# Attention's divisions, block turns and bias in another order, two heads turned by TensorE, and an MLP sum moved

## The chip, the cores and the metric

The kernel runs on one core of one Trainium2 chip. The metric is the device time in microseconds (us), median of several executions. TensorE (PE) multiplies, VectorE (DVE), ScalarE (ACT) and GpSimd (POOL) work element by element, and SyncE (SP) issues most transfers. POOL and ACT issue some too; transfers run on 16 shared engines.

## The reference, cut to what matters

A trunk of two layers on 512 tokens of width 1024. Each layer has a mixer and an MLP, each with a norm ahead of it and a residual addition behind.

```python
for layer in range(DEPTH):                       # DEPTH = 2
    hn = rmsnorm(h, norm_mix[layer])
    mix = attention(hn) if layer % 2 == 0 else rglru_block(hn)
    h = h + mix
    h = h + sq_relu_mlp(rmsnorm(h, norm_mlp[layer]), ...)   # relu(x @ w1)**2 @ w2
return rmsnorm(h, norm_final)

# attention: 16 heads of 64; a frame sees its own chunk of 64 and the 8 before it
s = einsum('bqhd,bkhd->bhqk', q_c, k_band) * scale + bias   # bias by clipped distance, per head
s = where(key_pos >= 0, s, NEG_INF)
p = softmax(s, axis=-1)
o = einsum('bhqk,bkhd->bqhd', p, v_band)                    # then o @ w_o
```

## The kernel before, in words

Everything is float32, and a product is made of three TensorE passes in float32r: each operand is split into a high part (a cast on ACT) and a low part (a subtraction on DVE), and high x high, high x low and low x high are added up in PSUM (`mm3`). So each weight tile that arrives costs ACT a cast `wh` and DVE a subtraction `wl` of 128 x 1024 before TensorE can use it.

Activations lie with channels in the partitions and the 512 tokens in the row. The program has three parts: attention (about the first 245 us), the first MLP, and the recurrent layer with the second MLP. The MLPs use sums of weight blocks and of activation blocks in place of one block product in eight; one such set of sums is `s1` to `s4` of a round.

In attention a head goes through these steps.
- `score(h)` (line 473): for four query tiles of 128, two matmuls each over the 128 to 512 keys up to the tile's end, into three PSUM banks; `K` and `Q` lie in both halves of the partitions, high part and low part, so that one pass of 128 rows gives two products. DVE adds the bias and takes the maximum (line 491), ACT takes the exponential and its sum (498), DVE the reciprocal, ACT divides (505).
- The block turn: DVE turns the 128 x 1280 probabilities in blocks of 32 x 32 (507), and sixteen transfers, eight on SP and eight on POOL (510), put the blocks where a full transpose would have them.
- `split_p(h)` (516): ACT casts the turned probabilities to the high part pH, DVE subtracts to get pL.
- `weigh(h)` (523): ten matmuls with V into one bank `oa`; ACT copies one half (`ax`), DVE adds (`o`); after the second head of a pair the pair is split into oH and oL.

Scores and `oa` take their banks from one set of four (`atp`), projections from another set of four (`mmp`).

What fills TensorE between heads is a queue of projections: V, the Q and K of pairs 2 to 7, and the output projection. Each is a generator that issues one `mm3` per step. `fill(n)` takes steps until a credit is used up, `need(name)` takes them until a projection is done. An entry of the queue may start only when a score or a weighting has been issued (`at["s"]`, `at["w"]`). `q_out` and `k_out` evacuate Q and K, and `k_out` copies the halves of K to the other partitions by four transfers on SP (kh and kl for two heads). The loop over `i` (617 to 641) issues score(i), a fill, split_p(i-2), weigh(i-3), a fill. A scheduler then sets the order on each engine from this, so the instruction order is not the order of the code.

The bias of four heads is one tile (373): one transfer of 512 KB, four copies and one memset on POOL.

In an MLP, `first` (797) runs the first up-projections, then calls `sums(0, False)`, `sums(0, True)` and `lengths()`; `sums(p, True)` makes the fourth sum of activations, s4, for the round, and `lengths` takes eight squared sums on ACT and four small instructions on DVE. `round_` (904) then takes its products in turn.

## Time and profile before

| | |
|---|---|
| median of 3 runs | 1033.38 us (1030.08 to 1033.62) |
| the profiled execution | 1030.76 us, span 1029.0 us |
| TensorE busy | 1006.7 us (98%), 5634 matmuls, mean granted clock 0.992 |
| VectorE busy | 865.8 us (84%) |
| ScalarE busy | 692.5 us (67%) |
| GpSimd busy | 163.4 us (16%) |
| mean HBM and on-chip transfer rate | 160 GB/s, 164.15 MB moved |

The span runs from the first to the last instruction; the execution is 1.8 us longer. Busy shares are averages over stages with different limits, so a stage is read by itself. A granted clock of 1.00 is TensorE's 2.4 GHz, of 0.50 its 1.2 GHz. A matmul counts as busy from its start to a modelled end, and matmuls overlap.

### The profile page before, as it was taken

To read this page: it belongs to the slowest core of one execution; us is meant where nothing else is said; L and a number is where in the kernel's file an instruction comes from. 1 tells how busy PE (TensorE), PEld (TensorE's weight loads), DVE (VectorE), ACT (ScalarE), POOL (GpSimd) and SP (SyncE) were. 2 spreads that over 40 slices of the span, in tenths; PEclk is the share of its full clock that TensorE was granted. 3 is DMA by queue.
4 is the path that set the end of the run, shared out by engine and by line. 5 is a ranking of instruction groups with operands and counts; after the bars stand their busy time and mean duration, and the time that the engine had idled before them with its cause. 6 is when DMAs were issued, how large, how long until landed. Compare 5 with 4: busy or idle time off the path is not lost.

```text
span 1029.0 us, 15661 instructions
## 1 busy us (share of the span) xinstructions
PE 1006.7 (98%) x5634; PEld 882.0 (86%) x5634; DVE 865.8 (84%) x1142; ACT 692.5 (67%) x1052; POOL 163.4 (16%) x256
## 2 busy tenths in 40 slices
PE   9998999979999999999999999999999999999997
PEld 8887788768989999999988788888999999999986
DVE  7899988759789898698688989987789798698687
ACT  7688988546786566567567686646686567567565
POOL 1053443313111111111020000003111111111020
PEclk9999999989999999999999999999999999999999
DMA  8476775549838738828673412186838838838572
GB/s 271 125 203 182 196 189 174 132 129 230 240 62 223 208 60 217 215 52 213 204 143 100 129 63 72 52 256 177 223 58 229 206 64 213 214 56 210 144 164 82
DMA packets 135725, 164.15 MB, mean 160 GB/s; under 512 B 10592, under 2 KB 102752, under 8 KB 135648
## 3 DMA queue, kind: packets, MB, share of 16 engines
q1 hardware_dynamic: 108896, 119.43, 37.4%
q0 software_dynamic: 26176, 43.01, 23.2%
q8 instruction: 44, 0.72, 0.3%
q10 hardware_dynamic: 576, 0.72, 0.2%
q14 instruction: 33, 0.27, 0.1%
HBM read 123.27 MB, written 2.10 MB: 122 GB/s over the span
## 4 chain that ended last, share of the span: by engine, by line
PE 75%; DVE 10%; ACT 6%; DMA 5%; issue 2%; SPq 1%; POOL 0%; DVEq 0%; ACTq 0%; POOLq 0%
PE m L290 8%; PE m L289 8%; PE m L288 8%; PE x L288 5%; PE x L289 5%; PE x L290 5%; PE y L289 4%; PE y L288 4%; PE y L290 4%; DVE wl L184 2%; DMA p<-pt 1%; DMA b<-in_w 1%; PE ro L290 1%; PE yb L290 1%; PE yb L288 1%
## 5 line engine op out<-in xcount | busy, mean ns | idle before, releaser
L184 DVE TENSOR_TENSOR wl<-b,wh 128x1024 fp32r<-128x1024 f32 x112 | 135.5, 1220 | 37.1 <-ACT wh L179 37.1
L179 ACT CAST wh<-b 128x1024 fp32r<-128x1024 f32 x112 | 116.7, 1051 | 61.5 <-PE m L289 19.1
L290 PE MATMUL m<-rH,wl 128*128 128x256 f32 x448 | 125.9, 281 | 0.0
L289 PE MATMUL m<-rL,wh 128*128 128x256 f32 x448 | 125.8, 281 | 0.0
L288 PE MATMUL m<-rH,wh 128*128 128x256 f32 x448 | 125.7, 281 | 0.0
L290 PE MATMUL m<-hnH,wl 128*128 128x256 f32 x336 | 95.0, 283 | 0.0
L289 PE MATMUL m<-hnL,wh 128*128 128x256 f32 x336 | 95.0, 283 | 0.0
L288 PE MATMUL m<-hnH,wh 128*128 128x256 f32 x336 | 94.9, 282 | 0.0
L179 ACT CAST wh<-wr 128x1024 fp32r<-128x1024 f32 (+1 forms) x65 | 66.6, 1028 | 38.1 <-PE ro L289 7.0
L289 PEld LDWEIGHTS m<-rL,wh 128*128 128x128 f32 x448 | 85.0, 190 | 1.2
L184 DVE TENSOR_TENSOR wl<-wr,wh 128x1024 fp32r<-128x1024 f32 (+1 forms) x66 | 77.9, 1184 | 9.3 <-ACT wh L179 9.0
L288 PEld LDWEIGHTS m<-rH,wh 128*128 128x128 f32 x448 | 84.8, 189 | 1.0
L290 PEld LDWEIGHTS m<-rH,wl 128*128 128x128 f32 x448 | 84.9, 189 | 0.0
L510 POOL DMA_DIRECT2D p<-pt x128 | 62.8, 499 | 121.8 <-DVE pt L507 70.1
L179 ACT CAST wh<-u 128x1024 fp32r<-128x1024 f32 x56 | 58.2, 1049 | 28.8 <-PE x L290 16.9
L184 DVE TENSOR_TENSOR wl<-u,wh 128x1024 fp32r<-128x1024 f32 x56 | 67.6, 1219 | 3.4 <-ACT wh L179 3.4
L289 PEld LDWEIGHTS m<-hnL,wh 128*128 128x128 f32 x336 | 64.3, 191 | 0.8
L288 PEld LDWEIGHTS m<-hnH,wh 128*128 128x128 f32 x336 | 64.2, 191 | 0.8
L290 PEld LDWEIGHTS m<-hnH,wl 128*128 128x128 f32 x336 | 64.3, 191 | 0.0
L136 POOL DMA_DIRECT2D kept<-in_w x14 | 18.3, 1308 | 261.0 <-DMA wr<-in_w 146.8
L163 POOL DMA_DIRECT2D u<-in_w x14 | 18.4, 1313 | 226.1 <-ACT m L853 117.2
L288 PE MATMUL x<-wh,h 128*128 128x512 f32 (+1 forms) x132 | 51.0, 386 | 0.6 <-DVE d L1062 0.6
(384 smaller groups left out, 3017.5 us busy)
## 6 DMA issues: line engine op xcount, KB each, us to landing
b<-in_w SPq DMA_DIRECT2D x68, 512.0 KB, 6.1
b<-b POOLq DMA_DIRECT2D x36, 512.0 KB, 6.5
kept<-in_w SPq DMA_DIRECT2D x28, 512.0 KB, 3.8
u<-in_w SPq DMA_DIRECT2D x28, 512.0 KB, 6.1
wr<-in_wqkv SPq DMA_DIRECT2D x20, 512.0 KB, 4.8
wr<-in_rwin SPq DMA_DIRECT2D x16, 512.0 KB, 3.6
kept<-in_w POOLq DMA_DIRECT2D x14, 512.0 KB, 7.2
u<-in_w POOLq DMA_DIRECT2D x14, 512.0 KB, 7.5
```

What stands on the lines that cost most here:

```text
L136: G.dma_start(four(raw), rows(upper[key]["22"]), accum_op=ALU.add)
L163: G.dma_start(four(raws["us3"]), rows(upper[key]["21"]), accum_op=ALU.add)
L179: high = S.copy(H[:, :n], raw[:, :n])
L184: low = V.tensor_sub(L[:, :n], raw[:, :n], f(H[:, :n]))
L288: PE.matmul(acc, WH, XH, start=start, stop=False, skip_group_check=more)
L289: PE.matmul(acc, WH, XL, start=False, stop=False, skip_group_check=more)
L290: PE.matmul(acc, WL, XH, start=False, stop=stop, skip_group_check=more)
L510: (G if j % 2 else nc.sync).dma_start(pt[32 * j : 32 * j + 32, i * 320 : (i + 1) * 320], turned[32 * i : 32 * i + 32, j].rearrange("p s a ...
```

## The change

Bias: a tile per head, with its own transfer, copy and memset; head i+3's is asked for in round i. In a round the order is now score(i), a fill, split_p(i-2), weigh(i-3), a fill, and then `divide(i)`: the division, the block turn and the sixteen transfers, which were part of `score` before. The last two heads (14 and 15) are divided on DVE and turned by ten TensorE transposes each (`turn`), and split out of PSUM; they are weighted by eight matmuls on the same number of columns. Q and K projections may start at any time, and their evacuation waits for the score that frees its buffers. The fill is 11.7 and later 7.5, where it was 11.5 and 8. The norm's accumulator moves to another tile. In the MLPs s4 and `lengths` are called behind the first product of the first round.

```diff
@@ -23,7 +23,7 @@
...
-FILL, LATE, LAG = 11.5, 8, 3
+FILL, LATE, TURNED = 11.7, 7.5, NH - 2
@@ -310,8 +310,7 @@
...
             if self.acc is None:
-                self.both = self.pool.tile([P, 2, T], F32, name=f"{self.name}acc", tag="nn")
-                self.acc = self.both[:, 0]
+                self.acc = self.pool.tile([P, T], F32, name=f"{self.name}acc", tag="o", bufs=1)
@@ -333,7 +332,7 @@
...
             PE.matmul(ss, ones.bitcast(F32R), aL, start=False, stop=True)
-            r = self.both[:, 1]
+            r = self.pool.tile([P, T], F32, name=f"{self.name}r", tag="nn")
@@ -370,13 +369,12 @@
...
-        def bias_of(g):
-            b = ab.tile([P, 4, T], F32, name=f"bias{g}", tag="bias")
-            nc.sync.dma_start(b[:, :, 2 * P :], win[4 * g : 4 * g + 4].rearrange("h p j -> p h j"))
-            for h in range(4):
-                G.tensor_copy(b[:, h, 0 : 2 * P], b[:, h, 2 * P : 2 * P + 1].to_broadcast([P, 2 * P]))
-            G.memset(b[0:HD, :, T - HD :], NEG)
-            biases[g] = b
+        def bias_of(h):
+            b = ab.tile([P, T], F32, name=f"bias{h}", tag="bias", bufs=4)
+            nc.sync.dma_start(b[:, 2 * P :], win[h])
+            G.tensor_copy(b[:, 0 : 2 * P], b[:, 2 * P : 2 * P + 1].to_broadcast([P, 2 * P]))
+            G.memset(b[0:HD, T - HD :], NEG)
+            biases[h] = b
@@ -409,6 +407,8 @@
...
                 yield 2
+            while at["s"] < 2 * p - 3:
+                yield 0
@@ -477,15 +477,15 @@
...
             sm = a2.tile([P, 4], F32, name=f"sm{h}", tag="sm")
-            b = biases[h // 4]
+            b = biases.pop(h)
...
                 n = (t + 1) * P
-                wide = pt[:, seg[t] : seg[t] + n], sc[t], b[:, h % 4, T - n :]
-                if t == 1:
+                wide = pt[:, seg[t] : seg[t] + n], sc[t], b[:, T - n :]
+                if t == 1 and h < TURNED:
@@ -500,6 +500,16 @@
...
             V.reciprocal(sm, sm)
+            pts[h] = pt, sm
+
+        def divide(h):
+            pt, sm = pts[h]
+            pts[h] = pt
+            if h >= TURNED:
+                for t in range(4):
+                    n = (t + 1) * P
+                    V.tensor_scalar(pt[:, seg[t] : seg[t] + n], pt[:, seg[t] : seg[t] + n], sm[:, t : t + 1], None, ALU.mult)
+                return
@@ -511,11 +521,28 @@
...
                     )
-            pts[h] = pt
+
+        def turn(h, pt, pH, pL):
+            x0, x1, x2 = atp(f"x0{h}"), atp(f"x1{h}"), atp(f"x2{h}")
+            dst = {(0, t): (x0, t * P) for t in range(4)}
+            dst.update({(1, t): (x1, (t - 1) * P) for t in range(1, 4)})
+            dst.update({(2, t): (x2, (t - 2) * P) for t in range(2, 4)})
+            dst[3, 3] = (x1, 3 * P)
+            for kt in (0, 1, 3, 2):
+                for t in range(kt, 4):
+                    b, c = dst[kt, t]
+                    PE.transpose(b[:, c : c + P], pt[:, seg[t] + kt * P : seg[t] + (kt + 1) * P], ident)
+            for b, c, n in ((x0, 0, T), (x1, T, T), (x2, 2 * T, 2 * P)):
+                S.copy(pH[:, c : c + n], b[:, :n])
+                V.tensor_sub(pL[:, c : c + n], b[:, :n], f(pH[:, c : c + n]))
...
             pH, pL = (a2.tile([P, 10 * P], F32R, name=f"p{n}{h}", tag=f"p{n}", bufs=1) for n in "HL")
+            if h >= TURNED:
+                turn(h, pt, pH, pL)
+                pHL[h] = pH, pL
+                return
@@ -524,14 +551,21 @@
...
             oa = atp(f"oa{h}")
-            for n, (kt, s0, s1, by, t) in enumerate(pieces):
+            todo = []
+            if h < TURNED:
+                for kt, s0, s1, by, t in pieces:
+                    x = oa.rearrange("p (s i a) -> p s i a", i=4, a=32)[:, t : t + len(range(s0, s1, by))]
+                    todo.append((kt, x, pL[:, s0:s1:by], pH[:, s0:s1:by]))
+            else:
+                for kt, (c, n) in enumerate(((0, 512), (512, 384), (1024, 256), (896, 128))):
+                    todo.append((kt, oa[:, T - n :], pL[:, c : c + n], pH[:, c : c + n]))
+            for n, (kt, x, L, H) in enumerate(todo):
                 vv = vt[p // 2][:, kt, p % 2, 2 * hh : 2 * hh + 2, :].rearrange("p s d -> p (s d)")
-                x = oa.rearrange("p (s i a) -> p s i a", i=4, a=32)[:, t : t + len(range(s0, s1, by))]
-                PE.matmul(x, vv, pL[:, s0:s1:by], start=n == 0, stop=False, skip_group_check=True)
-                PE.matmul(x, vv, pH[:, s0:s1:by], start=False, stop=n == 4, skip_group_check=True)
+                PE.matmul(x, vv, L, start=n == 0, stop=False, skip_group_check=True)
+                PE.matmul(x, vv, H, start=False, stop=n == len(todo) - 1, skip_group_check=True)
...
             if hh == 0:
-                oT[p] = a2.tile([P, T], F32, name=f"o{p}", tag="o", bufs=1)
+                oT[p] = ab.tile([P, T], F32, name=f"o{p}", tag="o", bufs=1)
@@ -576,12 +610,13 @@
...
                     mm3(acc, WH(k - k0, c), WL(k - k0, c), hnH[k], hnL[k], False, k == KT - 1)
-        bias_of(0)
+        for h in range(4):
+            bias_of(h)
...
         def qk(p):
-            return [(f"q{p}", qk_steps(p, q_out), ("s", 2 * p - 3)), (f"k{p}", qk_steps(p, k_out), ("s", 2 * p - 3))]
+            return [(f"q{p}", qk_steps(p, q_out), ("s", -1)), (f"k{p}", qk_steps(p, k_out), ("s", -1))]
@@ -595,14 +630,17 @@
...
             try:
-                credit[0] -= next(queue[0][1])
+                n = next(queue[0][1])
...
                 queue.pop(0)
+                return True
+            credit[0] -= n
+            return n > 0
...
             credit[0] = min(credit[0], 3) + n
-            while credit[0] > 0 and queue and at[queue[0][2][0]] >= queue[0][2][1]:
-                step()
+            while credit[0] > 0 and queue and at[queue[0][2][0]] >= queue[0][2][1] and step():
+                pass
@@ -614,11 +652,22 @@
...
         credit[0] = 0
-        for i in range(NH + LAG):
+        def weigh_at(h):
+            if h == 13:
+                need("woA")
+            need(f"v{h // 8}")
+            weigh(h)
+            if h == 7:
+                residual("h")
+                for k in range(KT):
+                    nc.sync.dma_start(hT[k], xT[k * P : (k + 1) * P, :])
+            at["w"] = h
+
+        for i in range(NH + 2):
...
             if i < NH:
-                if i % 4 == 0 and i > 0:
-                    bias_of(i // 4)
+                if 0 < i < NH - 3:
+                    bias_of(i + 3)
@@ -626,19 +675,17 @@
...
             fill(n)
-            if 0 <= i - LAG + 1 < NH:
-                split_p(i - LAG + 1)
-            if 0 <= i - LAG < NH:
-                if i - LAG == 13:
-                    need("woA")
-                need(f"v{(i - LAG) // 8}")
-                weigh(i - LAG)
-                if i - LAG == 7:
-                    residual("h")
-                    for k in range(KT):
-                        nc.sync.dma_start(hT[k], xT[k * P : (k + 1) * P, :])
-                at["w"] = i - LAG
+            if 0 <= i - 2 < NH - 2:
+                split_p(i - 2)
+            if 0 <= i - 3 < NH - 2:
+                weigh_at(i - 3)
             fill(n)
+            if i < NH:
+                divide(i)
+            if i >= NH:
+                split_p(i - 2)
+                fill(n)
+                weigh_at(i - 2)
@@ -815,8 +862,6 @@
...
                 sums(0, False)
-                sums(0, True)
-                lengths()
@@ -938,6 +983,9 @@
...
                 step("11", X, True, 0, 0)
+                if p == 0:
+                    sums(0, True)
+                    lengths()
```

At three places the scheduler's order stands like this. Names: kh20 is the high part of K of pair 2, first head; kl71 the low part of pair 7, second head; p2 are head 2's probabilities, pt2 their turned blocks; wr, weights that arrive.

On SP's queue, around the copies of K of pair 2, in the kernel before:

```order
L154 DMA wr18_1051<-in_wqkv 128x8x128
L510 DMA p1_589<-pt1_614 32x320 x8
L375 DMA bias1_905<-in_win 128x4x256
L401 DMA kh20_767<-kh20_767 64x512
L401 DMA kh21_773<-kh21_773 64x512
L510 DMA p2_679<-pt2_704 32x320 x8
L402 DMA kl20_768<-kl20_768 64x512
L402 DMA kl21_774<-kl21_774 64x512
L154 DMA wr19_1109<-in_wqkv 128x8x128
```

and in the changed one:

```order
L154 DMA wr18_980<-in_wqkv 128x8x128
L520 DMA p1_603<-pt1_690 32x320 x8
L374 DMA bias6_819<-in_win 128x256
L154 DMA wr19_1091<-in_wqkv 128x8x128
L399 DMA kh20_763<-kh20_763 64x512
L400 DMA kl20_764<-kl20_764 64x512
L399 DMA kh21_769<-kh21_769 64x512
L400 DMA kl21_770<-kl21_770 64x512
L374 DMA bias7_936<-in_win 128x256
L520 DMA p2_715<-pt2_801 32x320 x8
```

The four copies of K stand ahead of head 2's eight block transfers, where two of them stood behind.

On SP's queue, around the copies of K of pair 7, in the kernel before:

```order
L510 DMA p12_1888<-pt12_1913 32x320 x8
L401 DMA kh70_2090<-kh70_2090 64x512
L510 DMA p13_1956<-pt13_1981 32x320 x8
L402 DMA kl70_2091<-kl70_2091 64x512
L401 DMA kh71_2096<-kh71_2096 64x512
L402 DMA kl71_2097<-kl71_2097 64x512
L154 DMA wr32_2309<-in_wo 128x4x256
```

and in the changed one:

```order
L520 DMA p12_1925<-pt12_1972 32x320 x8
L154 DMA wr32_2306<-in_wo 128x4x256
L520 DMA p13_1993<-pt13_2068 32x320 x8
L399 DMA kh70_2127<-kh70_2127 64x512
L400 DMA kl70_2128<-kl70_2128 64x512
L399 DMA kh71_2133<-kh71_2133 64x512
L400 DMA kl71_2134<-kl71_2134 64x512
L154 DMA wr33_2340<-in_wo 128x4x256
```

All four copies stand behind the eight transfers of head 13, where the first stood ahead of them, and a weight transfer has come in between heads 12 and 13.

On DVE, at the end of attention (pL14 is the low part of head 14's probabilities, o7 the output of the last pair, oL7 its low part, x014 to x214 the banks of TensorE's transposes), in the kernel before:

```order
L437 TENSOR_TENSOR h1_1698<-wo07_2361,h1_1698 128x512
L184 TENSOR_TENSOR wl34_2431<-wr34_2432,wh34_2430 128x1024
L507 STREAM_TRANSPOSE pt15_2198<-p15_2173 128x10x4x32
L520 TENSOR_TENSOR pL14_2260<-p14_2105,pH14_2259 128x1280
L537 TENSOR_TENSOR o6_2231<-oa13_2375,ax13_2386 64x512
L542 TENSOR_TENSOR oL6_2390<-o6_2231,oH6_2389 128x512
L537 TENSOR_TENSOR o7_2408<-oa14_2397,ax14_2409 64x512
L520 TENSOR_TENSOR pL15_2394<-p15_2173,pH15_2393 128x1280
L537 TENSOR_TENSOR o7_2408<-oa15_2412,ax15_2423 64x512
L542 TENSOR_TENSOR oL7_2427<-o7_2408,oH7_2426 128x512
```

and in the changed one:

```order
L437 TENSOR_TENSOR h1_1744<-wo07_2358,h1_1744 128x512
L571 TENSOR_TENSOR o6_2244<-oa13_2372,ax13_2383 64x512
L537 TENSOR_TENSOR pL14_2391<-x014_2392,pH14_2390 128x512
L537 TENSOR_TENSOR pL14_2391<-x114_2393,pH14_2390 128x512
L576 TENSOR_TENSOR oL6_2387<-o6_2244,oH6_2386 128x512
L537 TENSOR_TENSOR pL14_2391<-x214_2394,pH14_2390 128x256
L184 TENSOR_TENSOR wl34_2462<-wr34_2463,wh34_2461 128x1024
L571 TENSOR_TENSOR o7_2420<-oa14_2411,ax14_2421 64x512
L537 TENSOR_TENSOR pL15_2425<-x015_2426,pH15_2424 128x512
L537 TENSOR_TENSOR pL15_2425<-x115_2427,pH15_2424 128x512
L537 TENSOR_TENSOR pL15_2425<-x215_2428,pH15_2424 128x256
L571 TENSOR_TENSOR o7_2420<-oa15_2445,ax15_2454 64x512
```

The block turn of head 15 is gone, and each of the two heads' splits is made in three parts, with a weight split and the pair's additions between them.

## Rows read from the trace of the kernel before

**Rows 1.** The page's first part: busy us, share of the span, instructions.

```profile
PE 1006.7 (98%) x5634; PEld 882.0 (86%) x5634; DVE 865.8 (84%) x1142; ACT 692.5 (67%) x1052; POOL 163.4 (16%) x256
```

**Rows 2.** Busy time by engine in four long stretches: stretch, its length, then busy us (and instructions) of PE, PEld, DVE, ACT and POOL, the granted TensorE clock, DMA share, GB/s.

```profile
26.00:60.00 34.00, 34.00 (x159) 28.50 (x158) 28.78 (x62) 23.47 (x46) 4.11 (x8) 1.00 0.56 147
60.00:130.00 70.00, 65.68 (x334) 55.54 (x333) 65.86 (x129) 62.99 (x129) 32.56 (x66) 1.00 0.70 191
290.00:300.00 10.00, 9.33 (x65) 8.45 (x64) 9.95 (x14) 9.10 (x11) 1.29 (x1) 1.00 0.26 63
300.00:1029.00 729.00, 721.29 (x4206) 638.07 (x4204) 617.08 (x722) 467.82 (x629) 74.60 (x78) 1.00 0.59 151
```

**Rows 3.** What TensorE waited for, over the whole span: waiting tile and line, releaser, total us, times, longest.

```profile
PE oa L530 <- DVE pL L520: 3.6, 1, 3.6
PE s L483 <- DMA kl<-kl: 3.4, 2, 1.7
PE s L483 <- issue: 1.6, 1, 1.6
PE s L483 <- DVE mx L491: 1.0, 1, 1.0
```

**Rows 4.** Busy time by engine in short windows around TensorE's waits; columns as in rows 2.

```profile
77.80:79.60 1.80, 0.13 (x2) 0.11 (x1) 1.80 (x2) 1.69 (x3) 0.30 (x3) 1.00 0.66 151
100.00:102.00 2.00, 0.96 (x5) 0.48 (x4) 1.94 (x5) 1.85 (x3) 0.98 (x2) 1.00 0.99 352
118.00:120.20 2.20, 0.59 (x4) 0.20 (x2) 2.15 (x5) 2.15 (x3) 1.01 (x3) 1.00 1.03 321
158.00:160.00 2.00, 0.88 (x8) 0.67 (x6) 1.89 (x3) 0.50 (x3) 2.00 (x6) 1.00 0.72 169
187.70:189.50 1.80, 0.09 (x2) 0.05 (x1) 0.58 (x1) 0.00 (x0) 0.00 (x0) 1.00 0.67 155
189.50:194.20 4.70, 4.70 (x23) 4.57 (x24) 1.90 (x9) 2.00 (x7) 0.00 (x0) 0.64 1.00 294
217.90:226.40 8.50, 2.81 (x12) 2.43 (x11) 2.21 (x3) 2.45 (x3) 0.00 (x0) 0.70 0.00 0
226.40:231.30 4.90, 4.90 (x12) 3.84 (x13) 2.44 (x4) 1.51 (x2) 0.00 (x0) 0.50 0.62 203
```

**Rows 5.** Instructions in order of time around the scores of heads 4 and 14: start us, us, engine, line, what, count, and in brackets the idle time ahead.

```profile
79.52 0.30 PE L483 MATMUL s<-kl,q 128*128 128x128 f32 x1 [1.67 <-DMA kl<-kl]
...
179.45 1.51 DVE L507 STREAM_TRANSPOSE pt<-p 128x1280 f32<-128x1280 f32 x1 [1.12 <-ACT p L505]
...
181.75 5.18 SPq L510 DMA_DIRECT2D p<-pt  x8
...
187.04 0.53 SPq L402 DMA_DIRECT2D kl<-kl  x1
...
189.48 0.30 PE L483 MATMUL s<-kl,q 128*128 128x128 f32 x1 [1.71 <-DMA kl<-kl]
```

**Rows 6.** The same at the end of attention.

```profile
211.85 4.99 SPq L510 DMA_DIRECT2D p<-pt  x8
...
218.79 1.26 ACT L519 CAST pH<-p 128x1280 fp32r<-128x1280 f32 x1 [2.91 <-DMA p<-pt]
...
221.63 0.58 PE oa L530
...
226.39 2.08 PE L288 MATMUL wo<-oH,wh 128*128 128x512 f32 x4 [2.04 <-ACT oH L541]
```

**Rows 7.** The chain of work that ended last, at the end of the first MLP: start us, us, what; 512-column matmuls and TensorE's transposes of the kernel before.

```profile
552.95 0.23 PE x L289
...
553.41 0.87 PE back L997 x8
```

**Rows 8.** The instructions on the tile that those transposes write: least, median and greatest ns, first and last start.

```profile
L997 PE MATMUL back<-ident,d x32: 270/272/329, 553.2 to 563.9; 128*128 128x128 f32 x32
```

**Rows 9.** Busy time by engine in the 13 us in which all 32 of them lie; columns as in rows 2.

```profile
553.00:566.00 13.00, 12.74 (x71) 10.16 (x70) 11.94 (x17) 10.91 (x21) 0.00 (x0) 1.00 0.54 167
```

**Rows 10.** Groups of instructions by line and shape: busy us, mean ns of one, idle time ahead and what ended it. The reduction has four widths, of which the widest and the narrowest are shown.

```profile
L491 DVE CUSTOM_DVE_ANT_0 p<-s,bias 128x512 f32<-128x512 f32 x16 | 11.0, 686 | 0.1
...
L491 DVE CUSTOM_DVE_ANT_0 p<-s,bias 128x128 f32<-128x128 f32 x16 | 4.6, 285 | 2.7 <-PE s L484 2.0 <-POOL bias L378 0.5
...
L520 DVE TENSOR_TENSOR pL<-p,pH 128x1280 fp32r<-128x1280 f32 x16 | 23.9, 1493 | 7.4 <-ACT pH L519 4.8 <-DMA p<-pt 1.5 <-DMA wr<-in_w 1.0
...
L437 DVE TENSOR_TENSOR h<-wo,h 128x512 f32<-128x512 f32 x16 | 10.6, 684 | 4.1 <-PE wo L290 4.0
...
L184 DVE TENSOR_TENSOR wl<-wr,wh 128x1024 fp32r<-128x1024 f32 x62 | 75.1, 1216 | 9.3 <-ACT wh L179 9.0
...
L1162 DVE TENSOR_SCALAR t<-t 128x512 f32<-128x512 f32 x8 | 3.4, 421 | 0.0
```

**Rows 11.** The chain of work that ended last, at a head's four exponentials and at the end of the first MLP's first group: start us, us, what.

```profile
44.47 2.29 ACT p L498 x8
...
292.62 1.12 DVE wl L184
...
293.78 0.50 PE y L289
```

## The prediction, made before the changed kernel had run

> **What bounds the kernel now.** I read the page's first part, then the busy time of TensorE by stretches, then what it waits for, then the instructions in order of time around each wait. TensorE is busy 1006.7 of 1029.0 us [rows 1], so all that can be won is its idle time, and the time in which it runs at a low clock. In a stretch of 70 us in the middle of attention it is idle for 4.3 us, around 290 us for 0.7; in the 729 us from 300 on for 7.7 [rows 2], but there the change touches only a few instructions in the second MLP. The list of waits names holders [rows 3]: score matmuls that wait for the copied half of K, for the reduction of an earlier head, or for something not shown; weighting matmuls (oa) that wait for the split probabilities pL.
>
> Short windows price each place in attention [rows 4]. Idle: 1.67 at 78; 1.04 at 100; 1.61 at 118; 1.12 at 158; 1.71 at 188; 5.69 from 217.9 to 226.4. Low clock: behind the wait at 188, TensorE works 4.70 us at a mean 0.64, which full speed does in 3.0: 1.7 lost. Between 217.9 and 226.4 its 2.81 us of work come after 221.6 [rows 6], at the 1.2 GHz level: 1.4 lost; the 4.90 behind, at 0.50, lose 2.45. The clock fell only behind the waits at 188 and 218 and stayed at 2.4 GHz in the other windows. Idle 12.8, with the MLP's 0.7 13.5, and 5.55 of low clock: 19.1 is the most that there is.
>
> **The change, part by part.** This execution took 1030.76, and the sum is made against that. The runs shown lie from 1030.08 to 1033.62 with the median 1033.38: it is a fast one, 2.6 below the median.
>
> *K's halves of pair 2.* Before, the copy kl20 stands on SP's queue behind eight block transfers of head 2, and the score of head 4 begins at 79.52 after 1.67 idle [rows 3 to 5]. In the new order the four K copies stand ahead of those eight. The wait goes: 1.7 won, at worst nothing. (Head 2's transfers are later for it; over 100 matmuls of 0.23 [rows 7], some 23 us, lie between its score and its oa.)
>
> *Bias per head, and scores of heads 7 and 9.* Head 9's 1.61 follows from head 8's first reduction, late behind the group's bias work on POOL and then cut in two by a block turn; head 7's 1.04 from a reduction cut in the same way. Now a head's bias is asked for three heads ahead, with one copy and one memset on POOL, and the block turn belongs to the end of the head's round. DVE is busy 65.9 of 70 us here [rows 2], so something can stay: 2.0 of 2.65 won, bounds 0 and 2.65. The bias transfers move the same bytes; the first four put two more SP issues of 0.6 ahead of V's weights, at a time when TensorE has other work without a gap [rows 2]: 0, and 1.2 if that cover is gone.
>
> *oa of head 8* waits for DVE to evacuate V (1.12). Three weight splits still stand ahead of it on DVE. 0.5 won, bounds 0 and 1.1.
>
> *K's halves of pair 7.* A chain: block turn of head 13 (1.51), eight issues (5.18), then kl70 at 187.04, the score at 189.48 [rows 5]. In the new order kh70 too stands behind the eight (0.6 more), and a residual addition and a weight split stand ahead of the turn on DVE. From the end of the projection: the first residual tile's twelve matmuls 2.8, addition and split 1.9 [rows 10], turn 1.5, eight issues 5.0 [rows 6], kh70 0.6, kl70 to the score 2.4, and 0.1 between each: 14.6. TensorE has 61 output-projection matmuls there instead of 49: 14.0. A wait of 0.6 stays of 1.71, 1.1 won. Waits of 1.0 to 1.7 elsewhere left the clock at 2.4 GHz, so the 1.7 behind it goes too: 2.8; bounds 0 and 3.4.
>
> *Last two heads.* Before: turn, eight issues of 4.99, landing, pH, pL, and oa of head 15 at 221.63; then ax, addition, oH, and the output projection at 226.39 [rows 6]. Now DVE divides, TensorE turns ten blocks per head, and ACT and DVE split out of PSUM. Eight transposes in a row take 0.87 [rows 7], 0.109 each: 20 cost 2.2. The weighting has the same 1280 columns twice. I count from head 14's first score matmul. DVE: a start of 0.7, four reductions 1.9 [rows 10], exponentials on ACT 2.3 [rows 11], the division 1.3, pL of head 12 1.5, the o addition 0.7, small ones 0.3: 8.7. (The division's four widths hold 1280 elements; 512 take 0.42, so 1.05 in proportion and 1.7 at four times that; the other end is 2.7, four ordinary additions.) TensorE is there after two scores and an oa of 1.2 each (2560 columns, five times 0.23) and 19 matmuls, at 8.0, and needs the bank which that addition frees: 0.7 idle. Then DVE has reductions 1.9, oL 0.7, three residual additions 2.0, pL13 1.5, two o additions 1.4, a weight split 1.2, the division 1.3, and the first part of head 14's split 0.7: 19.5 with small ones. TensorE: oa12, 16 matmuls, oa13, ten transposes, 11 matmuls: 18.4. 1.1 idle. Head 15 follows with 8 matmuls, its transposes and oa14 between: 0.1. Behind oa15 ten matmuls (2.3) now stand against ax, addition and oH, where 2.04 was idle: 0. So of 5.69 idle and 3.85 of low clock, 9.5, there remain 2.2 + 1.9: 5.4 won. DVE has some 23 us of work in these 28, so the waits are the weak figure: bounds 0 and 7.3.
>
> *MLP's fourth sum and squares later.* In the first MLP DVE's weight split stands at 292.62 behind the fourth sum, and the matmul waits for it until 293.78 [rows 11]. The sum (1.2) and two squares on ACT go from in front of the weight splits: 0.7 won, bounds 0 and 0.7. In the second MLP there is no idle time at this place: 0. The squares now stand among ACT's casts; 0, since the reads that need them come a whole product later.
>
> The sum: 1.7 + 2.0 + 0.5 + 2.8 + 5.4 + 0.7 = 13.1. Against it stand waits that the new order makes and the old trace can't show: the old order made five of 1.0 to 1.7, so between 0 and 4 us, and I take 2. That gives 1030.76 - 11.1 = 1019.7 for an execution like this one and 1022.3 from the median. I say 1021.
>
> **The rivals.** *The middle gives nothing*: DVE, busy 94% there, binds, and a wait that is removed comes back a head later. The terms 1.7, 2.0 and 0.5 go: 1021 + 4.2 = 1025. Against it: at 78 and 118 what DVE waits for is a queue, not work.
>
> *The transposes are slow and hold the clock down.* One lasts 0.272 from start to end [rows 8]; if they did not overlap here they would cost 5.4 instead of 2.2, and if the stretch ran at 1.2 GHz its 3.85 would stay: the tail then gives 9.5 - 5.4 - 1.9 - 3.85 = -1.7 instead of 5.4: 1028. Against it: in 13 us in which the kernel already turns 32 blocks, the granted clock is 1.00 [rows 9]. The Trainium skill, "TensorE: Matmul & The Clock Gate", section "Part 4: PE-mode transpose", says that a transpose took about 275 ns in one kernel's context and that it does not count as activity for the full clock. By its 275 the twenty would cost 5.5, an estimate from that page; the trace agrees on the length of one (272 ns), not on the rate or the clock.
>
> *Nothing that can be measured*: the tail's waits on DVE are 3 us longer and pair 7's wait stays with its low clock: 11.1 - 3 - 2.8 = 5.3 or less, 1026 to 1031.
>
> *Slower*: DVE comes to head 14 with work left over. Each microsecond of it is one of waiting at oa12 or oa14, and behind a wait as long as that of 218 the clock falls again. The scores now come later in the program, with 65 filler matmuls behind the last one instead of 83. With 7 us of arrears the tail holds 2.2 + 1.9 + 7 + 3.9 = 15.0 against 9.5, and if the middle wins nothing either: 1030.8 + 5.5 - 2.8 - 0.7 + 2 = 1035. It decides from about 3 us of arrears if the middle wins nothing, from 7 if it does. For it: DVE is busy 84% of the span [rows 1]. Against: at 188 and 218 DVE is idle most of the time [rows 4], so it is not behind today.
>
> **How the numbers follow.** Forecast 0.55; the middle gives nothing 0.16; slow transposes 0.07; nothing that can be measured 0.15; slower 0.07. About 0.5% (5.2 us) is what a measurement of this kernel can tell from no change. Faster by more: the forecast, the first rival, and a third of the next two, 0.77. Slower: 0.07. Within: 0.16. The lower end is where all 19.1 go and only 2.2 are added, counted from the fastest run: 1030.1 - 16.9 = 1013. The upper end takes in the third rival: 1031.
>
> **What will show it.** No idle TensorE at the score of head 4, under 1 us at those of heads 7, 9 and 14; a granted clock near 1.00 behind the score of head 14 and behind oa of head 15; transposes 0.11 apart; the second MLP as long as before. I am wrong if DVE keeps TensorE waiting over 3 us between head 14's scores and the last output projection, if the clock falls there, or if the heads before 130 us take as long as now.

## The result and the profile after

The changed kernel took 1022.01 us (median of 4 runs, 1021.37 to 1023.03) beside 1032.83 for the kernel before (median of 4): 0.9905 of its time, 95% interval 0.9888 to 0.9921 (the two medians alone give 0.9895). The prediction said 1021, and faster. A repetition (e9 below) gave 0.9913 (0.9896 to 0.9930).

The profiled execution took 1023.03 us with a span of 1021.3. It is the slowest of its four, while that of the kernel before was 2.1 below its median. So the two spans differ by 7.7 us where the medians differ by 10.8; the traces are set against the 7.7. First the page's first part of the changed kernel, which answers to [rows 1]: busy us, share of the span, instructions.

```profile
PE 1005.6 (98%) x5650; PEld 880.6 (86%) x5650; DVE 865.6 (85%) x1152; ACT 688.3 (67%) x1048; POOL 157.7 (15%) x252
```

Busy time by engine in three long stretches, as in [rows 2]: stretch, length, then busy us (and instructions) of PE, PEld, DVE, ACT and POOL, granted clock, DMA share, GB/s. The second stretch begins earlier than in [rows 2], since the place of the MLP's wait, 293.8 before, comes at about 287 now.

```profile
60.00:130.00 70.00, 66.67 (x333) 56.05 (x332) 64.88 (x132) 59.22 (x124) 31.85 (x70) 1.00 0.76 197
280.00:300.00 20.00, 20.00 (x135) 18.48 (x134) 19.19 (x23) 15.43 (x21) 2.58 (x2) 1.00 0.40 73
300.00:1021.00 721.00, 713.77 (x4151) 630.69 (x4149) 608.53 (x714) 463.69 (x624) 73.28 (x77) 1.00 0.59 152
```

The middle of attention is idle for 3.3 us where it was 4.3; the wait in the first MLP is gone; from 300 on 7.2 of idle time stand against 7.7. What TensorE waited for, as in [rows 3]:

```profile
PE s L483 <- issue: 2.2, 2, 1.5
PE oa L564 <- DVE v L432: 1.7, 1, 1.7
PE oa L564 <- DVE o L571: 1.6, 2, 1.2
PE s L483 <- DMA kl<-kl: 1.5, 1, 1.5
```

The two waits of the first line, at the scores of heads 7 and 9 (1.50 and 0.66), have no releaser in the profile; in order of time each ends 0.1 us behind a reduction on DVE that a block turn held up. The 3.6 for pL, which was the wait of the last head, is no longer in the list. New is a weighting that waits for o (1.2 at head 3: the bank frees only when head 2's output has been added), and the one for V has grown. The instructions in order of time at two of these places: start us, us, engine, line, what, count, idle time ahead. The first three lines belong to head 8's weighting, the others to head 14's score.

```profile
155.90 3.90 DVE L184 TENSOR_TENSOR wl<-wr,wh 128x1024 fp32r<-128x1024 f32 x3 [0.76 <-ACT wh L179]
159.72 0.86 DVE L432 SCALAR_TENSOR_TENSOR v<-v,rt,v 128x256 fp32r<-128x256 f32 x2
160.63 0.35 PE L564 MATMUL oa<-pL,v 128*128 128x128 f32 x1 [1.74 <-DVE v L432]
...
185.41 4.97 SPq L520 DMA_DIRECT2D p<-pt  x8
190.48 0.55 SPq L399 DMA_DIRECT2D kh<-kh  x1
191.12 0.54 SPq L400 DMA_DIRECT2D kl<-kl  x1
...
193.56 0.30 PE L483 MATMUL s<-kl,q 128*128 128x128 f32 x1 [1.53 <-DMA kl<-kl]
```

Windows behind those two waits and over the last heads; columns as above.

```profile
160.60:164.30 3.70, 3.67 (x11) 3.09 (x12) 3.35 (x5) 2.73 (x5) 2.01 (x5) 0.54 0.96 322
193.50:200.00 6.50, 6.45 (x37) 5.85 (x38) 3.16 (x14) 3.59 (x10) 0.00 (x0) 1.00 0.94 264
209.00:218.00 9.00, 8.86 (x52) 7.25 (x50) 8.46 (x16) 4.52 (x10) 0.00 (x0) 1.00 0.33 91
218.00:235.00 17.00, 17.00 (x79) 14.00 (x78) 14.14 (x22) 8.42 (x12) 1.39 (x1) 1.00 0.86 241
```

V's evacuation stands behind three weight splits on DVE, and kl70, the copy for which head 14's score waits, behind eight block transfers on SP's queue. The clock now falls behind head 8's wait (0.54 over 3.7 us, 1.7 lost) and no longer behind head 14's score or at the end of attention [rows 4]. The twenty transposes, in the answer on the tile they write (least, median, greatest ns, first and last start):

```profile
L534 PE MATMUL x<-ident,p x20: 270/272/294, 208.7 to 215.1; 128*128 128x128 f32 x20
```

One lasts 272 ns as in [rows 8], but in order of time ten of them begin at 208.75 and the matmul behind them at 209.75: 0.10 us apart, at a granted clock of 1.00. The Trainium skill's 275 ns ("TensorE: Matmul & The Clock Gate", section "Part 4: PE-mode transpose") agrees with the length of one, not with their rate here.

### The profile page after: what moved, and what is told of

The parts are those of the page before. It is cut to its first block, busy times and chain, and to the rows that moved or that the text cites. A ratio compares the mean times of both kernels' runs of the same rounds, so it can differ in the third digit from the quotient of the medians.

```text
span 1021.3 us, 15665 instructions
## 1 busy us (share of the span) xinstructions
PE 1005.6 (98%) x5650; PEld 880.6 (86%) x5650; DVE 865.6 (85%) x1152; ACT 688.3 (67%) x1048; POOL 157.7 (15%) x252
## 4 chain that ended last, share of the span: by engine, by line
PE 82%; DVE 7%; ACT 4%; DMA 3%; issue 2%; SPq 2%; DVEq 0%; ACTq 0%; POOL 0%; POOLq 0%
PE m L290 9%; PE m L289 9%; PE m L288 9%; PE x L288 6%; PE x L289 6%; PE x L290 6%; PE y L288 4%; PE y L289 4%; PE y L290 4%; SPq L520 2%; PE ro L290 1%; PE yb L288 1%; PE yb L290 1%; PE u L290 1%; PE ro L289 1%
## 5 line engine op out<-in xcount | busy, mean ns | idle before, releaser
L520 POOL DMA_DIRECT2D p<-pt x112 | 55.0, 499 | 52.9 <-DVE pt L517 27.5
```

The lines of the kernel that those rows point to most:

```text
L520: (G if j % 2 else nc.sync).dma_start(pt[32 * j : 32 * j + 32, i * 320 : (i + 1) * 320], turned[32 * i : 32 * i + 32, j].rearrange("p s a ...
```

## The experiments

Two theories. *Tail*: the last two heads bring nearly all of the gain, and the rest of the change only moves waits in the middle. *Parts*: every term of the forecast brings about its share. For the middle there were two further ones: DVE's load binds there, or the order of what stands on DVE and ACT does.

The table sums up the twelve runs: ratio to the kernel before on the same chip, with its 95% interval, and TensorE's idle us in attention from 60 us on: the sum of its waits of 0.3 us or more, read in order of time, up to head 14's score, and behind it. The median of the kernel before differs from chip to chip (1031.9 us beside e1 to e4, 1030.4 beside e5 to e8, 1031.1 beside e9 to e11, 1032.2 beside e12), so runs are compared by their ratios.

| run | ratio | 95% | idle up to score 14 | idle behind |
|---|---|---|---|---|
| before | 1 | | 7.2 | 5.7 |
| changed | 0.9905 | 0.9888–0.9921 | 6.6 | 0.4 |
| e9 changed again | 0.9913 | 0.9896–0.9930 | 7.5 | 0.4 |
| e1 tail undone | 1.0019 | 1.0006–1.0032 | 5.5 | 9.8 |
| e2 tail alone | 0.9914 | 0.9896–0.9931 | 7.3 | 0 |
| e3 turn early | 0.9920 | 0.9903–0.9938 | 6.1 | 0.4 |
| e4 bias by group | 0.9943 | 0.9927–0.9959 | 11.0 | 0 |
| e5 gate undone | 0.9912 | 0.9896–0.9928 | 6.1 | 0.4 |
| e6 head 8 later | 0.9906 | 0.9889–0.9923 | 5.7 | 0.4 |
| e7 turn of 13 later | 0.9936 | 0.9911–0.9960 | 7.6 | 0 |
| e8 both | 0.9919 | 0.9901–0.9936 | 7.0 | 0 |
| e10 splits left out | 0.9919 | 0.9898–0.9940 | 6.3 | 0.4 |
| e11 splits on GpSimd | 0.9977 | 0.9964–0.9989 | 13.3 | 0 |
| e12 weigh first | 0.9932 | 0.9918–0.9947 | 7.2 | 0.5 |

**e1, the tail undone**

```diff
-FILL, LATE, TURNED = 11.7, 7.5, NH - 2
+FILL, LATE, TURNED = 11.7, 7.5, NH
...
-        for i in range(NH + 2):
+        for i in range(NH + 3):
...
```

> The changed kernel with one part undone: heads 14 and 15 go the old way (division on ACT, block turn on DVE, eight transfers, split). Theory (the last two heads carry most of the gain): the trace of the changed kernel has 2.2 us of transposes and 0.5 of waits there where 9.5 us of waits and low clock stood, so this run is some 6.8 us longer than the changed kernel's 1022.0: about 1029, with a wait of 3 to 6 us before the last weighting matmuls and a granted clock of about 0.5 behind it. By the forecast's own term 5.4: 1027.4. Rival (every part carries its share and the tail little, as slow transposes would make it): under 1024.

It took 1033.8 us: 0.19% more than the kernel before and, by the ratios, 1.06 to 1.14% (11 to 12 us) more than the changed kernel. TensorE's waits at the end of attention, in order of time:

```profile
214.16 0.39 PE L564 MATMUL oa<-pL,v 128*128 128x256 f32 x1 [1.14 <-DVE pL L547]
217.38 1.20 PE L288 MATMUL wo<-oH,wh 128*128 128x512 f32 x4 [1.18 <-ACT oH L575]
225.43 0.58 PE L564 MATMUL oa<-pL,v 128*128 128x256 f32 x1 [5.03 <-DVE pL L547]
230.19 1.22 PE L288 MATMUL wo<-oH,wh 128*128 128x512 f32 x2 [2.05 <-ACT oH L575]
```

9.4 us where the kernel before has 5.7 [rows 3, 6]. In this order 71 output-projection matmuls stand between head 14's score and head 15's weighting instead of 83; the 12 that are missing are 2.8 us (at 0.23 [rows 7]) less cover for the same transfers. In this execution the clock fell behind head 3's weighting too (0.51 from 103.7 to 110.7 us). So without the turn by TensorE the rest of the change does not win: it loses 2 us, with an interval that begins just above 1.

**e2, the tail alone**, in the kernel before (the division on DVE, `turn` itself and the eight weighting matmuls come with it, as in the changed kernel):

```diff
+            if h >= TURNED:
+                turn(h, pt, pH, pL)
...
-        for i in range(NH + LAG):
+        for i in range(NH + 2):
```

> The kernel before with this one part put in: the last two heads divided by DVE and turned by TensorE. Theory: 6.8 us less than the kernel before's 1032.8, so about 1026; the waits at heads 4, 7, 9, 8's weighting and 14 stay as they were (7.2 us of idle time before 200 us, and the 1.7 of low clock behind head 14's score). By the forecast's term 1027.4. Rival (the tail pays only because the division and the transfers of the earlier heads moved too): 1030 or more.

1023.1 us, 8.8 less than the 1031.9 of the kernel before on the same chip. Its waits, and its windows:

```profile
PE s L483 <- DMA kl<-kl: 3.5, 2, 1.9
PE s L483 <- issue: 1.6, 1, 1.6
PE oa L561 <- DVE v L432: 1.1, 1, 1.1
PE s L483 <- DVE mx L491: 1.1, 1, 1.1
```

```profile
60.00:130.00 70.00, 65.47 (x325) 55.45 (x324) 64.17 (x127) 61.27 (x127) 32.66 (x66) 0.98 0.70 186
190.00:240.00 50.00, 48.91 (x245) 41.11 (x246) 42.55 (x87) 29.69 (x52) 3.14 (x3) 1.00 0.60 172
275.00:295.00 20.00, 20.00 (x126) 18.05 (x126) 17.07 (x21) 17.53 (x29) 1.28 (x1) 1.00 0.27 53
```

All the old waits of the middle are there as in [rows 3], those at the end are gone, and the last output-projection matmul ends at 235.6 us: 7.1 before that of the kernel before (242.7) and 0.4 before that of the changed kernel (236.0). This part alone does as well as the whole change (0.9914 beside 0.9905 and 0.9913). The MLP's wait of 0.67 is gone too (its place comes at about 286.7 here, in the last stretch), though the fourth sum stands where it stood; why was not tried. The low clock did not come behind head 14's wait of 1.69, but behind head 4's of 1.86 (0.72 from 79 to 85 us).

**e3, the turn early**

```diff
                 score(i)
+                divide(i)
...
-            if i < NH:
-                divide(i)
```

> The changed kernel with the division, block turn and transfers of a head back directly behind its exponentials. Theory (DVE is full between 75 and 160 us, and moving the turn only moved the waits): between 1021 and 1024, since the reductions cut by block turns lie elsewhere and cost as much; the wait for the copied half of K at head 4 stays away, because the order of the projections is as in the changed kernel. By the forecast (its terms of 1.7 for pair 2 and a part of the 2.8 for pair 7 rest on the turn being later): 1024 to 1026, with 1.7 us idle before head 4's score.

1024.2 us, its interval overlapping that of the changed kernel. There is no wait at head 4, so the later turn is not needed to take it away: kl20 is issued at 70.31, ahead of the block transfers. The other waits lie at other heads (1.63 at head 2's weighting, 0.98 at head 7's score, 1.30 at head 9's weighting).

**e4, the bias by group**

```diff
...
-        for h in range(4):
-            bias_of(h)
+        bias_of(0)
...
-                if 0 < i < NH - 3:
-                    bias_of(i + 3)
+                if i % 4 == 0 and i > 0:
+                    bias_of(i // 4)
```

> The changed kernel with the bias in one tile per four heads again, asked for at heads 4, 8 and 12. By the forecast's term of 2.0 for heads 7 and 9: 1024.0. Theory (the bias part won nothing net, because a wait at head 7 or 9 has its cause in DVE's load): 1022 to 1023, with a longer wait at the score of head 9 (1.6 us instead of 0.7) and shorter ones at heads 3 and 7.

1026.3 us, 0.9943: by the ratios 3.1 to 3.9 us more than the changed kernel. Its interval lies above that of the first series and overlaps that of the repetition by 0.0003. Theory and forecast both had it too low. DVE and GpSimd at head 4's first reduction, in order of time:

```profile
81.11 1.43 POOL L376 COPY bias<-bias 128x256 f32<-128x256 f32 x4 [2.85 <-DMA bias<-in_win]
82.48 0.30 POOL L377 MEMSET bias<- 64x256 f32 x1
82.82 0.29 DVE L492 CUSTOM_DVE_ANT_0 p<-s,bias 128x128 f32<-128x128 f32 x1 [1.83 <-DMA p<-pt]
```

DVE stands still until GpSimd has finished four copies and the memset (the profile names a transfer as the releaser, but the memset ends at 82.78). The reduction starts 1.5 us later than in the changed kernel (81.33 there), head 3's pL as well (102.07 against 100.62), and the waits at heads 2, 3, 6 and 8 grow. The kernel before has no such stall at this place, though its bias comes by group too: there the transfer is issued at 68.54 on SP, and the memset ends at 78.08, well ahead of the same reduction at 81.30. In e4 it is issued at 73.22, behind K's four copies. So e4 shows what a bias by group costs in the new order, not what it cost in the old one.

**e5, the gate undone**

```diff
-            while at["s"] < 2 * p - 3:
-                yield 0
...
-            return [(f"q{p}", qk_steps(p, q_out), ("s", -1)), (f"k{p}", qk_steps(p, k_out), ("s", -1))]
+            return [(f"q{p}", qk_steps(p, q_out), ("s", 2 * p - 3)), (f"k{p}", qk_steps(p, k_out), ("s", 2 * p - 3))]
```

> The changed kernel with the old gate for the projections of Q and K: a pair's first matmul, not its copies, waits for the score two heads earlier. Theory (it is this gate, not the later block turn, that took away the wait at head 4, since the run with early turns had none there): the wait for kl20 of about 1.7 us comes back at the score of head 4, and the time is 1023.5 to 1025. Rival (the block turn behind the round is what keeps SP's queue free): no wait at head 4, about 1022.

1021.6 us, 0.9912. No wait came back at head 4. There is one of 1.69 at head 5's score, but it is not for K:

```profile
71.55 1.19 SPq L400 DMA_DIRECT2D kl<-kl  x2
81.99 0.42 DVE L489 CUSTOM_DVE_ANT_0 p<-s,bias 128x256 f32<-128x256 f32 x1
82.52 0.30 PE L481 MATMUL s<-kl,q 128*128 128x128 f32 x1 [1.69 <-issue]
```

K's copies are issued by 72.74, ahead of the block transfers, and the score starts 0.1 us behind head 4's second reduction, which stood behind a block turn (80.38 to 81.88). The rival was right. Together with e3: with the rest of the change, either the opened gate or the later turn is enough to keep K's copies ahead. The sum of waits is 0.5 lower, and the time the same.

**e6, head 8 later**

```diff
+            if h == 8:
+                for _ in range(5):
+                    step()
             weigh(h)
```

> The changed kernel with fifteen matmuls of pair 7's Q projection put between the last V matmul and the weighting of head 8. Theory (the 1.74 us at that weighting is V's evacuation behind three weight splits on DVE, and the 1.7 us of low clock behind it is its consequence): both go, 3.4 us won, about 1018.6, granted clock 1.00 from 150 to 180 us. Rival (DVE is behind there, and the wait comes back at the weighting of head 9 or the score of head 13): 1021 to 1022.

1020.7 us, 0.9906: the wait for V and the low clock behind it are gone from the trace (granted 1.00 from 150 to 180), and 1.41 came back at head 9's weighting. So 0.9 us of waits and 1.7 of low clock went, and the span of the profiled execution is 1018.8, 2.5 less; but the intervals overlap, and in the repeated run of the changed kernel other executions took as little as 1021.8. A gain is not shown.

**e7 and e8, head 13's turn later**

```diff
+                if i == 14:
+                    divide(13)
             fill(n)
...
-            if i < NH:
+            if i < NH and i != 13:
                 divide(i)
```

> The changed kernel with the division, block turn and transfers of head 13 behind the score of head 14, so that pair 7's four K copies stand ahead of the eight block transfers on SP's queue. Theory (the 1.53 us at head 14's score is the queue): the wait goes, 1.5 us won, about 1020.5. Rival (the transfers of head 13 then come too late): a wait of over 1 us at the weighting of head 13, 1022 or more.

> The last two runs' edits together. If each takes away a wait of its own: 1022.0 - 3.4 - 1.5 = 1017.1. If the two share the same spare time of DVE: 1018.5 to 1020.

1022.7 and 1022.2 us (0.9936 and 0.9919; two of e7's six executions took 1026.7 and 1028.5). The four K copies do stand ahead of head 13's transfers now, but in e7 the score also comes 19 matmuls earlier, and it waits 1.81 (2.02 in e8). There was no new wait at head 13's weighting. So neither theory holds: the copies came earlier, and so did the score that needs them.

**e9 to e11, DVE's load in the middle**

```diff
-        L = wsp.tile([P, 1024], F32R, name=f"wl{i}", tag="wl")
+        L = H if 18 <= i < 28 else wsp.tile([P, 1024], F32R, name=f"wl{i}", tag="wl")
...
-        low = V.tensor_sub(L[:, :n], raw[:, :n], f(H[:, :n]))
+        if not 18 <= i < 28:
+            low = V.tensor_sub(L[:, :n], raw[:, :n], f(H[:, :n]))
```

and, in e11, `(G if 18 <= i < 28 else V).tensor_sub(...)`.

> The changed kernel itself once more, on the chip of the two runs below, to set them against it directly and to see whether its 1.74 us wait at the weighting of head 8 and the low clock behind it are there in another execution. Expected: 0.989 to 0.992 of the kernel before, and the wait again; the low clock only in some executions.

> The changed kernel without the weight splits of ten weight tiles (18 to 27, those of pair 6, of V's second half, of pair 7's Q and of the first output projections): their high part stands in for the low part, so 12 us of DVE work between 85 and 160 us are left out, and TensorE's work is the same. Theory (DVE's load binds between 90 and 165 us): the 1.17, 1.50, 0.66 and 1.74 us of waits there shrink to under 1.5 in all, and the time falls by 3.5 to 5 us with the low clock behind 160: about 1018. Rival (the waits come from the order of instructions, a block turn in front of a reduction, not from the load): they stay within 1 us of 5.1 in all, and the time is 1021 to 1022.

> The same ten weight splits computed by GpSimd instead of DVE, so nothing is left out. If GpSimd, busy 15%, takes them beside its DMA issues without slowing DVE, the result is that of the run that leaves them out: about 1018. If GpSimd's copies are a guide (256 columns in 0.4 to 0.75 us, so 1.6 to 3 us for 1024), a split is late by 1 to 2 us, which the weights' lead of several tiles hides. Rival: block transfers queued behind a split on GpSimd come later, or DVE slows beside it: 1022 or more, with new waits at the weightings for pL.

e9 took 1022.2, e10 1022.5: 12 us of DVE work less, and nothing won. The waits at heads 3, 7, 9 and 8's weighting are 4.84 us in all, 5.07 in the changed kernel. From 90 to 110 us, the changed kernel's window and then e10's:

```profile
90.00:110.00 20.00, 17.33 (x88) 14.15 (x87) 19.68 (x38) 17.07 (x34) 8.20 (x19) 1.00 0.71 191
```

```profile
90.00:110.00 20.00, 17.44 (x88) 14.25 (x87) 17.59 (x35) 18.06 (x37) 8.35 (x19) 1.00 0.72 186
```

DVE falls from 98% to 88%, TensorE's idle time from 2.67 to 2.56. In order of time in e10:

```profile
96.74 0.40 ACT L499 ACTIVATE p<-p,mx 128x128 f32<-128x128 f32 x1 [0.86 <-DVE mx L496]
...
98.94 1.25 ACT L547 CAST pH<-p 128x1280 fp32r<-128x1280 f32 x1
...
99.07 0.18 DVE L503 RECIPROCAL sm<-sm 128x4 f32<-128x4 f32 x1 [0.98 <-ACT p L499]
100.22 1.49 DVE L548 TENSOR_TENSOR pL<-p,pH 128x1280 fp32r<-128x1280 f32 x1 [0.97 <-ACT pH L547]
```

Head 3's pL waits for pH on ACT, which stands behind head 5's exponentials, which wait for head 5's maximum on DVE, which stands behind head 2's pL. From one pL to the next (89.66 to 100.22) this round takes 10.6 us; in the changed kernel it is 10.7 (89.91 to 100.62), and the weight splits lay in its gaps. So the load that these splits make does not bind. The rest of DVE's work is another matter: from 89.66 to 96.65 DVE works in this chain almost without a gap, and no run left any of that out.

At head 8 the order changed as well. Without the three weight splits V is ready 1.4 us sooner (159.25 against 160.63), and DVE now stands idle for ACT's part of V's evacuation, which stands on ACT between weight casts and a division:

```profile
158.71 0.48 DVE L433 SCALAR_TENSOR_TENSOR v<-v,rt,v 128x256 fp32r<-128x256 f32 x1 [1.11 <-ACT v L432]
159.25 0.33 PE L565 MATMUL oa<-pL,v 128*128 128x128 f32 x1 [1.47 <-DVE v L433]
```

But TensorE comes there 1.1 sooner too, with five score matmuls fewer ahead, and the wait is 1.47. In e11 a split takes twice as long on GpSimd as on DVE (1.22):

```profile
L184 POOL TENSOR_TENSOR wl<-wr,wh 128x1024 fp32r<-128x1024 f32 x10 | 24.2, 2432 | 6.5 <-ACT wh L179 6.5
```

and it took 1028.4, with 3.77 idle at head 3's weighting and 6.10 at head 8's (the profiled execution, 1031.5, is the slowest of the twelve). At head 3:

```profile
97.52 4.73 POOL L184 TENSOR_TENSOR wl<-wr,wh 128x1024 fp32r<-128x1024 f32 x2
99.80 4.14 DVE L547 TENSOR_TENSOR pL<-p,pH 128x1280 fp32r<-128x1280 f32 x1 [0.98 <-ACT pH L546]
103.86 0.67 DVE L571 TENSOR_TENSOR o<-oa,ax 64x512 f32<-64x512 f32 x1
104.59 0.58 PE L564 MATMUL oa<-pL,v 128*128 128x256 f32 x1 [3.77 <-DVE o L571]
```

The same pL takes 1.49 in e10. Beside GpSimd's splits it takes 2.65 longer, the addition behind it comes as much later, and the wait of 1.06 in e10 becomes 3.77. So of the rival's two causes, DVE slowing down beside GpSimd is shown here; at head 8 DVE's part of V waits for ACT, as in e10, and what makes that wait so long was not tried.

**e12, weigh first**, on top of e6's edit

```diff
+            if 0 <= i - 3 < NH - 2:
+                weigh_at(i - 3)
             if 0 <= i - 2 < NH - 2:
                 split_p(i - 2)
-            if 0 <= i - 3 < NH - 2:
-                weigh_at(i - 3)
```

> The run that puts fifteen matmuls before the weighting of head 8, with one more edit: in a head's round the weighting of an earlier head is written ahead of the next head's split instead of behind it. No work is added or left out. On DVE the scheduler then puts both reductions that read a head's first score bank ahead of the block turn, where the turn stood between them before. Theory (after the run without ten weight splits: what binds in the middle is the order on DVE and ACT, not their load): the wait of 1.4 to 1.5 us at the score of head 7 shrinks to under 0.3, that at the third head's weighting stays about 1.2, and the time is 1.0 to 1.5 us under that of the run it is built on, 0.989 of the kernel before. Rival (load binds after all, and the turn's 1.5 us come back at the next wait): the idle time before 165 us stays at 4.5 to 5 us, and the time is the same.

1025.2 us, 0.9932. Head 3's wait fell to 0.31, head 7's first to 0.48 with 1.14 behind it, where the block turn now stands. Head 9's weighting waits 3.77 for its pL:

```profile
162.47 1.05 ACT L179 CAST wh<-wr 128x1024 fp32r<-128x1024 f32 x1 [2.70 <-DMA wr<-in_wo]
163.42 0.47 ACT L431 ACTIVATE v<-v,rt 128x256 fp32r<-128x256 f32 x1
165.92 1.26 ACT L546 CAST pH<-p 128x1280 fp32r<-128x1280 f32 x1
168.97 0.39 PE L564 MATMUL oa<-pL,v 128*128 128x256 f32 x1 [3.77 <-DVE pL L547]
```

In this order a weight cast stands on ACT ahead of ACT's last part of V and of pH, and ACT is idle for 2.70 until, by the profile, that weight has landed; in e6 that part of V stands ahead of the cast. So order does decide where TensorE waits; this order is worse in sum. None of the runs is measurably better than the changed kernel.

## Why the prediction was right

The time and the sign are right; the sum behind them is right only because two misses cancel. By medians the last two heads with the MLP gave 8.8 (e2) where the sum has 6.1, and the rest gave 0 to 2 (the whole is 8.9 in the repetition and 10.8 in the first series) where the sum has 7.0 less the reserve of 2. That these misses are about as large is luck. Of the signs named ahead, no idle at head 4's score, 0.66 at head 9's, the clock behind head 14's score and at the end, and transposes 0.10 apart came; the waits under 1 us at the scores of heads 7 and 14 did not (1.50 and 1.53).

*Last two heads, 5.4.* Right in mechanism, too small. The 2.2 for twenty transposes held. The waits that I put at 1.9 were 0.5: DVE was there in time at both places (0.39 at head 12's weighting, 0.14 at head 14's). The bound of 7.3 was the better value: the end of attention moved by 6.7 us in the changed kernel and by 7.1 with this part alone. Between medians it is 8.8 alone, with the MLP's 0.7, and 11 to 12 on top of the rest: the traces set an execution of the kernel before that lies 2.1 below its median, and in e1 the old way also pays for the 12 matmuls that went.

*Pair 2, 1.7.* Right: the wait went, and because K's copies stand ahead (issued by 73.3 us instead of 78.3). By e3 and e5 two parts of the change each do that. It gave no time that can be seen: heads 3 and 7 wait longer instead.

*Bias and heads 7 and 9, 2.0.* Failed as a term: 2.65 became 1.17 + 1.50 + 0.66 = 3.33. The step that failed: the block turn, now at the end of a round, was to stand no longer between a head's reductions. At head 7 it still does, and the score starts 0.1 us behind the second reduction:

```profile
104.10 0.29 DVE L491 CUSTOM_DVE_ANT_0 p<-s,bias 128x128 f32<-128x128 f32 x1
104.32 1.51 DVE L517 STREAM_TRANSPOSE pt<-p 128x1280 f32<-128x1280 f32 x1
105.75 0.39 DVE L491 CUSTOM_DVE_ANT_0 p<-s,bias 128x256 f32<-128x256 f32 x1
106.25 0.30 PE L483 MATMUL s<-kl,q 128*128 128x128 f32 x1 [1.50 <-issue]
```

The bias part is needed in the new order (e4), but the stall of 1.83 that it avoids there is one that the old order did not have (0.5 in all [rows 10]).

*Head 8, 0.5.* Failed: 1.12 became 1.74 and cost 1.7 of clock. The three weight splits did stand ahead; in the repetition it was 2.22. By e10 they are not the whole cause: without them V waits for ACT's part of its evacuation.

*Pair 7, 2.8.* The clock's 1.7 came, the wait stayed at 1.53 where I had 0.6. I counted 4.8 from the end of the projection to the block turn; it took 5.8 (178.04 to 183.88): some 0.7 because a subtraction for Q stood ahead of the addition on DVE (180.97 to 181.66), and 0.36 because the turn waited for head 13's division on ACT, behind a weight cast. My chain left out both.

*MLP, 0.7.* The wait is gone, but it is gone in e2 without that edit, so it is not shown that the edit is what took it away.

*The reserve of 2 for new waits* was too small: of the middle's 7.0 (1.7, 2.0, 0.5 and 2.8) the traces show 0.6, idle time of 6.6 instead of 7.2, and the 1.7 of low clock only moved from head 14 to head 8. The rival "the middle gives nothing" describes what happened there. Its cause, as I had it, was DVE's load; by e10 that does not hold for the weight splits. That the round between ACT and DVE sets the waits is read from the rows. It fits e4 and e10, and e11, where a pL that took longer came back in full as waiting; but no run shortened that round alone, so it is not shown. The other rivals fell: the transposes were neither slow nor at a low clock, and no arrears of DVE came to head 14.

## What to carry to other kernels

Price a wait by the chain that ends there, around all its in-order queues, not by the busy share of the engine named last: DVE, 98% busy, gave up ten weight splits (12 us) that lay outside the chain, and nothing was won; a pL inside the chain that took 2.65 longer (e11) lengthened the wait behind it by 2.7. The waits at the end of attention, with nothing queued behind them, were won nearly in full, less the price of the transposes; those in the middle of the loop mostly came back at another head. Before a wait is called the old one come back, see in order of time what it waits for (e5). Take the parts of a change apart before believing the terms of a sum that came out right; and a part taken out of the new order (e4) need not cost what it would have brought in the old one.

## What the runs showed of the hardware

The length of a wait alone did not tell whether the clock falls behind it. Behind 1.74 at head 8 the granted clock was 0.54 for 3.7 us, behind 1.74 at head 3 (e1) 0.51 for 7.0, behind 1.86 at head 4 (e2) 0.72 over 6; behind 1.99 at head 8 (e7) and 2.16 at head 3's weighting (e4) it stayed at 1.00. The forecast, that waits up to 1.7 leave it alone, was only a description of one trace.

A subtraction of 1024 columns took 2.43 us on GpSimd and 1.22 on DVE. Beside such splits on GpSimd (e11) some of DVE's instructions took far longer: pL 4.14 us instead of 1.49, two subtractions for K 2.75 and 2.91 instead of 0.69, a small one on 128 x 4 3.20 instead of 0.16. Reductions that read scores and block turns beside them took as long as ever (0.55 for 384 columns, 1.51).
